# The RMS norm of the memory tokens: spread over partitions by VectorE and a matmul with ones in place of a round trip through DRAM

## The chip, the cores and the metric

The kernel runs on one core of one Trainium2 chip. The metric is the device time of one execution in microseconds (us). Three runs of the kernel before took 786.47, 784.92 and 788.44 us; their median is 786.47 us.

The engines of the core go by the names that the profile gives them: PE is TensorE (matmuls; PEld are its weight loads), DVE is VectorE, ACT is ScalarE, POOL is GpSimd and SP is SyncE. SP and POOL issue most of the DMAs. Each engine works through its own instructions in their order, and waits at one until what it needs is there; waits between engines are semaphores.

## The reference

One block of a hybrid decoder on 512 tokens of width 1024 in float32: a token mixer (SSD heads and causal pooling), a cross-attention into 256 memory tokens, a SwiGLU feed-forward, each with an RMS norm ahead and a residual add behind, and a last RMS norm. What the change touches is the norm of the memory tokens, `rmsnorm(mem, mem_norm)`, which feeds the keys and values of the cross-attention:

```python
def rmsnorm(x, g):
    xf = x.astype(jnp.float32)
    y = xf * lax.rsqrt(jnp.mean(xf * xf, axis=-1, keepdims=True) + EPS)
    return (y * g.astype(jnp.float32)).astype(x.dtype)
...
    k, v = jnp.split(m_in @ w_kv, 2, axis=-1)
...
        h = h + memory_cross_attention(rmsnorm(h, xattn_norm[l]), rmsnorm(mem, mem_norm[l]),
                                       w_q[l], w_kv[l], w_o[l])
```

## The kernel before, in words

**Number format.** Each operand of a large product is split in two parts, a rounded high part (`whi`, `t_xh`, the left half of `t_mn`) and the rest (`wlo`, `t_xl`, the right half of `t_mn`). A product is then three matmuls: high by high, high by low, low by high. For a weight chunk, ScalarE (or VectorE, for chunks named in `FLAGS`) casts the high part (line 282) and VectorE subtracts to get the low part (line 290). The chunks lie in rotating buffers: six for raw weights (`raw`), four for `whi`, five for `wlo`, two each for two kinds of `wq`.

**Strassen products.** The output projection of the mixer's SSD half is one of the products that are computed by seven sub-products f = 1 to 7. Items `y:f` are these; each has two weight chunks of two k-pairs, and 24 matmuls (line 1384) into PSUM tiles `yA`, `yB` or `yC`. Some weights are sums of quadrants. For y:3 the sum is made by DMAs that POOL issues with an add (`sums`, lines 220 and 223): line 223 adds `wq` into `wq`, and the result is what line 282 casts for y:3.

**The order.** `SPEC` is a list of slots, written by hand. Each slot names items. The main loop goes over the slots: for slot t it emits the `post` part of the items of slot t-1, the `prep` part of those of slot t+1, the weight splits for slot t+1, and then the matmuls (`mm`) of slot t. A scheduler orders what it emits on each engine, TensorE in the order of emission.

**The memory tokens.** Two items: `ml` (`i_memld`, line 1118) loads `mem` by rows (`t_rmx`) and its transpose (`t_mem`, eight tiles of 128 channels by 256 tokens), squares the rows on ScalarE with a sum per token, and calls `RmsT.split` (line 434), which makes 1/rms for each token as a column `rm` (128 x 2: token on partition). The transposed tiles need that number along the free dimension, equal on all partitions (`t_rmt`, 128 x 256). With the flag `rmdma`, `split` gets it through DRAM: one DMA writes the column to `d_rm` (line 443), and a second reads it back, broadcast over the partitions (line 445). Both are issued by SP, which also issues the weight loads; the second waits for the first. Without the flag, the rest of `split` and `mm` and `post` of the same class do it on the engines, as they do for `r1`, the norm of the first stage.

The item `mm` (`i_mem`, line 1134) then scales each of the eight tiles (line 1142, VectorE), casts the high part (line 156, ScalarE) and subtracts for the low part (line 157, VectorE) into `t_mn`. `k:1` (`i_k`, line 1172, matmuls of lines 1182 and 1183) is the first product that reads `t_mn`. Its second weight, k.3, gets its low part by a POOL DMA (line 242).

The slots around it are, in order, `y:2.1`, an empty one, `y:5.1 y:6`, `y:3 mm`, `k:1`. So the scaling is emitted with the slot of `k:1`.

The branches of `RmsT` that matter:

```python
            if self.base + "dma" in FLAGS:
                d = dram.tile([n, P], F32, name="d_" + self.base)
                nc.sync.dma_start(d.rearrange("c p -> p c"), p)
                t = self.rt = T(self.base + "t", n=n * P)
                nc.sync.dma_start(t, d.rearrange("c p -> (c p)").unsqueeze(0).broadcast_to([P, n * P]))
                return
            self.rd = T("rd", n=n * P)
            st["spread", self.base] = nc.vector.tensor_tensor(
                                    out=self.rd.rearrange("p (c l) -> p c l", l=P),
                                    in0=ident.unsqueeze(1).broadcast_to([P, n, P]),
                                    in1=p.unsqueeze(2).broadcast_to([P, n, P]), op=ALU.mult)
```

Of the kernel before, what the change touches and what calls it, by code (L numbers as in the profile page):

```python
# [42 lines left out]
START_MM = "10 20 00 11 21 01 12 22 02 13 23 03 24 14 04 15 25 05 16 26 06 17 27 07 a r b c"  # L43

HOLD = 3
FLAGS = ('rmdma', 'Ck.4', 'Ck.3', 'D5.1', 'Cv.2', 'Cv.0', 'Ck.0', 'Cz.6', 'Cz.3', 'D0.0', 'Cz.7', 'D6.1', 'Ck.7', 'yd3', 'D1.1', 'Cv.3', 'yd4', 'Cz.1', 'Cv.4', 'Cq.5', 'Cq.4', 'Cz.5', 'Cq.3', 'Cxbc.11', 'D6.0')
DMA_KEYS = ('q.6', 'xbc.11', 'q.7', 'z.7', 'z.5', 'k.3', 'q.3', 'z.2', 'z.4', 'z.3')
REST = ('g1', 'g0')

# [31 lines left out]
def hybrid_block(ctx: ExitStack, tc: tile.TileContext, a: dict, out: bass.AP,  # L81
# [163 lines left out]
    def split_unit(key):  # L245
# [28 lines left out]
        if key[0] == "s" and f == (6 if CHUNKS[c][0] == "d" else 5):  # L274
            sw[c, "drained"] = st["first rest"] if f == 6 else st.get("drained")
        behind = key[0] == "xbc" and ("free" not in FLAGS or key != plan[1]) and ("spread", "r1") in st
        if "C" + ".".join(str(k) for k in key) in FLAGS:
            cast = nc.vector.tensor_copy(hi[:, :n], raw[:, :n])
# [80 lines left out]
    class Rms:  # L359
# [19 lines left out]
        def mm(self):  # L379
            n = self.n  # L380
            self.ps = PS(self.base)
            if self.parts:
                for i in range(2):
                    nc.tensor.matmul(self.ps[:, :n], ones_r, self.src[i], start=i == 0, stop=i == 1)
            else:
                nc.tensor.matmul(self.ps[:, :n], ones, self.src, start=True, stop=True)

        def post(self):
            n, base, ps = self.n, self.base, self.ps
            y = T(base + "y", n=n)  # L390
            ln = nc.scalar.activation(y, ps[:, :n], AF.Ln, bias=eps)
            after(ln, self.pre)
            nc.scalar.activation(y, y, AF.Exp, scale=-0.5)
            yield
            t = T(base + "t", n=n)
            nc.vector.scalar_tensor_tensor(out=t, in0=ps[:, :n], scalar=eps, in1=y, op0=ALU.add, op1=ALU.mult)
            nc.vector.scalar_tensor_tensor(out=t, in0=t, scalar=-0.5, in1=y, op0=ALU.mult, op1=ALU.mult)
            nc.vector.scalar_tensor_tensor(out=t, in0=t, scalar=1.5, in1=y, op0=ALU.add, op1=ALU.mult)
            st[base,] = t
# [18 lines left out]
    class RmsT:  # L418
# [15 lines left out]
        def split(self):  # L434
# [5 lines left out]
            yield  # L440
            if self.base + "dma" in FLAGS:
                d = dram.tile([n, P], F32, name="d_" + self.base)
# [10 lines left out]
        def mm(self):  # L453
            if self.base + "dma" in FLAGS:
                return
# [3 lines left out]
        def post(self):  # L459
            if self.base + "dma" in FLAGS:  # L460
                st[self.base,] = self.rt
# [6 lines left out]
    def sq_acc(name, src, n=512):  # L468
# [4 lines left out]
        else:  # L473
            sq = T("sq", n=n)
            st[name, "sq"] = nc.scalar.activation(sq, src, AF.Square)
            if f"yd{count[name]}" in FLAGS:
                nc.gpsimd.dma_start(st[name], sq, accum_op=ALU.add)
# [1365 lines left out]
```

## Time and profile before

| what | value |
|---|---|
| median of three runs | 786.47 us |
| the profiled execution | 787.49 us |
| its span, first to last instruction | 785.8 us |
| mean granted TensorE clock | 0.993 |
| HBM read, written | 120.20 MB, 2.13 MB |

The profile is one execution. Its times count from the start of the span. In rows of the timeline the first number is the start in us, the second the duration in us, then engine, line, operation, output and inputs by the program's names, shape and count; in brackets stands the idle time of the engine just ahead, with what ended it. Matmuls are pipelined, so a duration of 0.39 us can stand beside a pace of 0.23 us; the pace is read from the starts. In a row of the view by stretches the busy times of PE, PEld, DVE, ACT and POOL follow the length of the stretch, and behind them stand the granted clock of TensorE, the share of the 16 DMA engines and GB/s.

### The profile page before, as it was taken

To read this page: it belongs to the slowest core of one execution; us is meant where nothing else is said; L and a number is where in the kernel's file an instruction comes from. 1 tells how busy PE (TensorE), PEld (TensorE's weight loads), DVE (VectorE), ACT (ScalarE), POOL (GpSimd) and SP (SyncE) were. 2 spreads that over 40 slices of the span, in tenths; PEclk is the share of its full clock that TensorE was granted. 3 is DMA by queue.
4 is the path that set the end of the run, shared out by engine and by line. 5 is a ranking of instruction groups with operands and counts; after the bars stand their busy time and mean duration, and the time that the engine had idled before them with its cause. 6 is when DMAs were issued, how large, how long until landed. Compare 5 with 4: busy or idle time off the path is not lost.

```text
span 785.8 us, 10551 instructions
## 1 busy us (share of the span) xinstructions
PE 773.9 (98%) x3734; PEld 647.8 (82%) x3734; DVE 646.2 (82%) x1028; ACT 509.3 (65%) x816; POOL 77.6 (10%) x103
## 2 busy tenths in 40 slices
PE   9999999999999989999999999999999999999996
PEld 7788888888888778888888878888888888888985
DVE  5889979989698787667898897789876789867887
ACT  7688788665767356466585597575455666454865
POOL 1000000100001000120210101001101011111010
PEclk9999999999999989999999999999999999999999
DMA  9555743442579886878965966857889786789622
GB/s 331 192 160 151 187 144 93 122 138 84 160 266 240 132 276 195 182 177 257 264 133 126 243 141 190 181 166 159 225 213 270 177 247 156 214 221 244 165 55 107
DMA packets 46676, 145.04 MB, mean 185 GB/s; under 512 B 5472, under 2 KB 7840, under 8 KB 46624
## 3 DMA queue, kind: packets, MB, share of 16 engines
q1 hardware_dynamic: 33952, 100.52, 37.1%
q0 software_dynamic: 12384, 43.52, 31.4%
q8 instruction: 29, 0.48, 0.2%
q10 hardware_dynamic: 288, 0.33, 0.1%
q14 instruction: 23, 0.19, 0.1%
HBM read 120.20 MB, written 2.13 MB: 156 GB/s over the span
## 4 chain that ended last, share of the span: by engine, by line
PE 92%; DVE 4%; DMA 2%; issue 1%; ACT 1%; SPq 0%; DVEq 0%; ACTq 0%
PE gA L1384 15%; PE gB L1384 8%; PE dA L1384 6%; PE gC L1384 4%; PE dB L1384 3%; PE oA L1384 3%; PE xbc L142 2%; PE xbc L141 2%; PE xbc L143 2%; PE vAB L1384 2%; PE k L1182 2%; PE z L141 2%; PE z L143 2%; PE q L141 2%; PE v L141 2%; PE z L142 2%
## 5 line engine op out<-in xcount | busy, mean ns | idle before, releaser
L290 DVE TENSOR_TENSOR wlo<-raw,whi 128x1024 fp32r<-128x1024 f32 (+1 forms) x107 | 128.0, 1206 | 41.9 <-ACT whi L282 40.6
L282 ACT CAST whi<-wq 128x1024 fp32r<-128x1024 f32 (+1 forms) x96 | 99.1, 1034 | 74.9 <-PE gA L1384 11.8
L290 DVE TENSOR_TENSOR wlo<-wq,whi 128x1024 fp32r<-128x1024 f32 (+1 forms) x96 | 114.0, 1199 | 35.4 <-ACT whi L282 34.5
L282 ACT CAST whi<-raw 128x1024 fp32r<-128x1024 f32 x96 | 98.7, 1036 | 60.2 <-PE gA L1384 10.2
L1384 PE MATMUL gA<-whi,t_xh 128*128 128x512 f32 (+1 forms) x240 | 81.4, 373 | 0.0
L1384 PE MATMUL gA<-wlo,t_xh 128*128 128x512 f32 (+1 forms) x192 | 71.4, 372 | 0.0
L202 POOL DMA_DIRECT2D raw<-w_s x42 | 37.1, 884 | 303.0 <-DMA raw<-w_s 209.0
L1384 PE MATMUL gA<-whi,t_xl 128*128 128x512 f32 (+1 forms) x144 | 53.5, 371 | 0.0
L1384 PEld LDWEIGHTS gA<-whi,t_xh 128*128 128x128 f32 x240 | 44.6, 188 | 7.8
L1384 PEld LDWEIGHTS gA<-wlo,t_xh 128*128 128x128 f32 x192 | 36.2, 188 | 6.2
L1384 PE MATMUL gB<-whi,t_xh 128*128 128x512 f32 (+1 forms) x96 | 36.0, 375 | 0.0
L1384 PE MATMUL gB<-wlo,t_xh 128*128 128x512 f32 (+1 forms) x96 | 35.7, 372 | 0.0
L1384 PE MATMUL gB<-whi,t_xl 128*128 128x512 f32 (+1 forms) x96 | 35.7, 371 | 0.0
L1384 PE MATMUL dA<-whi,t_xl 128*128 128x512 f32 (+1 forms) x91 | 34.8, 382 | 0.0
L1384 PE MATMUL dA<-wlo,t_xh 128*128 128x512 f32 (+1 forms) x91 | 34.8, 382 | 0.0
L1384 PE MATMUL dA<-whi,t_xh 128*128 128x512 f32 (+1 forms) x91 | 34.5, 382 | 0.0
L220 POOL DMA_DIRECT2D wq<-raw x22 | 19.7, 895 | 145.8 <-DVE wlo L290 117.7
L1384 PEld LDWEIGHTS gA<-whi,t_xl 128*128 128x128 f32 x144 | 27.1, 189 | 4.6
L1400 ACT ACTIVATE t_gu<-t_gu,r 128x512 f32<-128x512 f32 (+1 forms) x24 | 16.3, 687 | 20.5 <-DVE t_gu L1396 20.5
L141 PE MATMUL z<-t_uh,whi 128*128 128x512 f32 x64 | 25.2, 393 | 0.0
L141 PE MATMUL op<-whi,t_pgh 128*128 128x512 f32 x64 | 25.1, 393 | 0.0
L141 PE MATMUL v<-t_uh,whi 128*128 128x512 f32 x64 | 25.0, 391 | 0.0
(445 smaller groups left out, 2218.3 us busy)
## 6 DMA issues: line engine op xcount, KB each, us to landing
raw<-w_s SPq DMA_DIRECT2D x62, 512.0 KB, 4.8
raw<-w_u SPq DMA_DIRECT2D x52, 512.0 KB, 4.1
wq<-w_s SPq DMA_DIRECT2D x44, 512.0 KB, 4.8
raw<-w_s POOLq DMA_DIRECT2D x40, 512.0 KB, 7.2
wq<-raw POOLq DMA_DIRECT2D x21, 512.0 KB, 6.3
wlo<-raw POOLq DMA_DIRECT2D x10, 512.0 KB, 6.4
wq<-wq POOLq DMA_DIRECT2D x9, 512.0 KB, 8.5
t_abc<-d_acs SPq DMA_DIRECT2D x16, 256.0 KB, 4.6
```

Of the source, the lines that this page charges most:

```text
L141: nc.tensor.matmul(ps, whi, xhi, start=start, stop=False)
L142: nc.tensor.matmul(ps, whi, xlo, start=False, stop=False)
L143: nc.tensor.matmul(ps, wlo, xhi, start=False, stop=stop)
L202: nc.gpsimd.dma_start(sw[c, f][:, :n], quad("11" if f == 7 else "22"), accum_op=ALU.add)
L220: nc.gpsimd.dma_start(sw[c, 6][:, :n], sw[c, 5][:, :n], accum_op=ALU.add)
L282: cast = nc.scalar.copy(hi[:, :n], raw[:, :n])
L290: rest = nc.vector.tensor_tensor(out=lo[:, :n], in0=raw[:, :n], in1=hi.bitcast(F32)[:, :n], op=ALU.subtract)
L1182: nc.tensor.matmul(it.ps[d], wh[:, ws], both, start=k == 0, stop=False, skip_group_check=True)
L1384: nc.tensor.matmul(it.ps[tt][:, o:e], p[:, ts_], w[:, ws], start=first, stop=(c, i, n) == pairs[-1] and p is xh and w is wl, skip_group_ch ...
L1400: st["silu"] = nc.scalar.activation(g, g, AF.Silu, scale=st["r3",][:, c:c + 1])
```

## The change

The flag `rmdma` goes, and the item `mm` moves one slot ahead, between y:5.1 and y:6:

```diff
-FLAGS = ('rmdma', 'Ck.4', 'Ck.3', 'D5.1', ...
+FLAGS = ('Ck.4', 'Ck.3', 'D5.1', ...
...
-    "yr y:2.0 y:5.0", "", "y:1.1", "y:2.1", "", "y:5.1 y:6", "y:3 mm", "k:1", "hg:2 hg:0", "", "k:0 y:7", "", "",
+    "yr y:2.0 y:5.0", "", "y:1.1", "y:2.1", "", "y:5.1 mm y:6", "y:3", "k:1", "hg:2 hg:0", "", "k:0 y:7", "", "",
```

Without the flag, `RmsT.split` ends in the VectorE product shown above (line 448: the identity matrix times the column, 128 x 256, into `t_rd`), and the item has a matmul and a copy of its own:

```python
        def mm(self):
            if self.base + "dma" in FLAGS:
                return
            self.ps = PS(self.base)
            nc.tensor.matmul(self.ps[:, :self.cols * P], ones, self.rd, start=True, stop=True)
...
            t = T(self.base + "t", n=self.cols * P)
            nc.scalar.activation(t, self.ps[:, :self.cols * P], AF.Copy, scale=float(DM))
```

On SP the two DMAs of the round trip stood between the weight loads of line 190, behind the last of the memory tiles' loads; they are gone, and the loads behind them follow the one ahead directly.

On TensorE, at the seam between y:5.1 (`yB`) and y:6 (`yA`), stands a new matmul of the ones with `t_rd`:

```order
L1384 MATMUL yB_2669<-whi_2731,t_xl_2574 128x512
L1384 MATMUL yB_2669<-wlo_2732,t_xh_2561 128x512
L457 MATMUL rm_2780<-t_rd_2592,ones 128x256
L1384 MATMUL yA_2598<-whi_2739,t_xh_2340 128x512
L1384 MATMUL yA_2598<-whi_2739,t_xl_2349 128x512
```

Nothing else moves on TensorE. On VectorE `t_rd` is made right behind the column it spreads, while `ry`, the norm of the mixer's output, is under way:

```order
L415 TENSOR_TENSOR rm<-rm 128x2
L290 TENSOR_TENSOR wlo_2698<-wq_2542,whi_2697 128x1024
L448 TENSOR_TENSOR t_rd_2592<-ident,rm 128x256
L412 TENSOR_TENSOR ry<-ry 128x4
L290 TENSOR_TENSOR wlo_2732<-raw_2544,whi_2731 128x1024
```

Row L448 is new, the others stand as before. Further on, VectorE's scaling of the tiles (L1142) keeps its place behind the adds of `yB`; of the eight tiles the fifth now comes ahead of the weight split for y:3 and the eighth ahead of the last three low parts. On ScalarE the copy out of PSUM (L464) stands ahead of the casts of `t_mn`, and the cast of y:3's second chunk (`whi_2764`) behind three of them, as before:

```order
L241 ACTIVATE wlo_2760<-raw_2729 128x1024
L240 CAST whi_2759<-raw_2729 128x1024
L464 ACTIVATE t_rmt_2807<-rm_2780 128x256
L156 CAST t_mn_2815<-t_mem_2522 128x256
L156 CAST t_mn_2821<-t_mem_2524 128x256
L156 CAST t_mn_2825<-t_mem_2526 128x256
L282 CAST whi_2764<-wq_2542 128x1024
```

Row L464 is the only new one.

More of the change, by code (lines that the diff above doesn't have):

```diff
@@ L45 @@
 HOLD = 3
-FLAGS = ('rmdma', 'Ck.4', 'Ck.3', 'D5.1', 'Cv.2', 'Cv.0', 'Ck.0', 'Cz.6', 'Cz.3', 'D0.0', 'Cz.7', 'D6.1', 'Ck.7', 'yd3', 'D1.1', 'Cv.3', 'yd4', 'Cz.1', 'Cv.4', 'Cq.5', 'Cq.4', 'Cz.5', 'Cq.3', 'Cxbc.11', 'D6.0')
+FLAGS = ('Ck.4', 'Ck.3', 'D5.1', 'Cv.2', 'Cv.0', 'Ck.0', 'Cz.6', 'Cz.3', 'D0.0', 'Cz.7', 'D6.1', 'Ck.7', 'yd3', 'D1.1', 'Cv.3', 'yd4', 'Cz.1', 'Cv.4', 'Cq.5', 'Cq.4', 'Cz.5', 'Cq.3', 'Cxbc.11', 'D6.0')
 DMA_KEYS = ('q.6', 'xbc.11', 'q.7', 'z.7', 'z.5', 'k.3', 'q.3', 'z.2', 'z.4', 'z.3')
```

## The prediction

> **What bounds the kernel now.** I read the page first, then the list of who waited on TensorE, then the chain of waits around the stage that is changed, and last the timeline of single instructions there.
>
> ```profile
> span 785.8 us, 10551 instructions
> PE 773.9 (98%) x3734; PEld 647.8 (82%) x3734; DVE 646.2 (82%) x1028; ACT 509.3 (65%) x816; POOL 77.6 (10%) x103
> PE 92%; DVE 4%; DMA 2%; issue 1%; ACT 1%; SPq 0%; DVEq 0%; ACTq 0%
> ```
>
> TensorE (PE) is busy for 98% of the span and is 92% of the chain that ended last. So a change counts only where it makes TensorE stop, run slower, or do more work. The second view lists all its stops; its columns are the total, the number of times and the longest.
>
> ```profile
> PE yB L1384 <- ACT whi L282: 2.0, 1, 2.0
> PE warm L549 <- DVE ones L120: 1.2, 1, 1.2
> PE yB L1384 <- DVE wlo L290: 0.7, 1, 0.7
> PE hT L1541 <- DVE t_h L1331: 0.2, 1, 0.2
> ```
>
> Four stops in all. The two at yB are neighbours, in the item y:3, and they are the only ones that are not the start or 0.2 us. The chain of waits shows what stands behind them (start, duration, what).
>
> ```profile
> 257.90 8.47 DMA d_rm<-rm
> 266.42 7.46 DMA t_rmt<-d_rm
> 273.90 1.28 DVE t_mem L1142 x3
> 275.18 0.51 DVE t_h L1079
> 275.76 1.09 DVE t_mn L157 x3
> 276.85 0.40 DVE t_mem L1142
> 277.24 1.15 DVE wlo L290
> 278.43 6.34 PE yB L1384 x16
> ```
>
> The memory norm goes out to DRAM and comes back in 15.9 us; VectorE scales the first memory tokens only at 273.90, and behind those the second weight chunk of y:3 is cast late. This is the DMA's 2% of the whole chain. Now what it costs TensorE, from its timeline; each row is one matmul, and those left out follow at an even pace.
>
> ```profile
> 267.68 0.39 PE L1384 MATMUL yA<-whi,t_xh 128*128 128x512 f32 x1
> 273.12 0.39 PE L1384 MATMUL yB<-whi,t_xh 128*128 128x512 f32 x1
> 276.62 0.68 PE L1384 MATMUL yB<-whi,t_xh 128*128 128x512 f32 x1 [1.97 <-ACT whi L282]
> 284.61 0.40 PE L1182 MATMUL k<-t_mn,whi 128*128 128x512 f32 x1
> 287.39 0.39 PE L1182 MATMUL k<-t_mn,whi 128*128 128x512 f32 x1
> 276.77:283.60 6.83, 6.12 (x14) 4.34 (x15) 6.33 (x13) 2.95 (x6) 0.83 (x1) 0.50 0.99 226
> ```
>
> y:6 (yA) has 24 matmuls and takes 273.12 - 267.68 = 5.44 us, 0.227 us each. y:3 (yB) has 24 of the same shape and takes 284.61 - 273.12 = 11.49 us. **The loss is 11.49 - 5.44 = 6.05 us.** The last row, of the view by stretches, explains the larger part: from 276.77 to 283.60 the granted clock (third number from the end) is 0.50. The stops are 2.7 us of the loss; the other 3.4 us are y:3 at half pace.
>
> **The change part by part.** *TensorE gets one matmul more*, rm<-t_rd,ones 128x256, ahead of y:6. The same form runs once at the start, with 512 columns, between even matmuls.
>
> ```profile
> 24.02 0.39 PE L143 MATMUL xbc<-t_xgh,wlo 128*128 128x512 f32 x1
> 24.25 1.02 PE L457 MATMUL r<-t_rd,ones 128*128 128x512 f32 x2
> 24.71 0.80 PE L141 MATMUL xbc<-t_xgh,whi 128*128 128x512 f32 x1
> 25.34 0.40 PE L142 MATMUL xbc<-t_xgl,whi 128*128 128x512 f32 x1
> ```
>
> Without r the row at 25.34 would start two even steps after 24.02, at 24.48; so r costs 0.86 us. I take half of it for half the columns, **+0.43 us**; ends 0.23 (one even matmul) and 0.86.
>
> *VectorE and ScalarE get one instruction each*: t_rd (L448) and the copy out of PSUM (L464).
>
> ```profile
> L448 DVE TENSOR_TENSOR t_rd<-ident,r x1: 692/692/692, 22.8 to 22.8; 128x512 f32<-128x512 f32 x1
> L464 ACT ACTIVATE t_r1t<-r x1: 600/600/600, 25.3 to 25.3; 128x512 f32<-128x512 f32 x1
> 259.56 0.17 DVE L412 TENSOR_TENSOR ry<-ry 128x4 f32<-128x4 f32 x1 [0.56 <-ACT ry L411]
> 267.65 1.06 ACT L240 CAST whi<-raw 128x1024 fp32r<-128x1024 f32 x1 [0.71 <-PE yB L1384]
> 268.10 1.40 DVE L1079 SCALAR_TENSOR_TENSOR t_h<-yB,ry,t_h 128x512 f32<-128x512 f32 x2
> 274.42 1.20 ACT L156 CAST t_mn<-t_mem 128x256 fp32r<-128x256 f32 x3 [5.71 <-DVE t_mem L1142]
> 275.52 1.04 ACT L282 CAST whi<-wq 128x1024 fp32r<-128x1024 f32 x1
> ```
>
> At half the size they take between 0.35 and 0.69, and 0.30 and 0.60 us. t_rd stands just ahead of L412 and so falls into the 0.56 us for which VectorE waits there: cost 0 to 0.13 us on VectorE, nothing on TensorE, which needs t_rd 8 us later. L464 stands behind L240, in 5.7 us of idle ScalarE. Both cost nothing; if that cover were gone it would be at most 0.7 us in the chain below.
>
> *The wait that goes.* rm's matmul runs at 267.68; L240 ends at 268.71, L464 by 269.3, and VectorE has finished its adds at 269.50. So the first t_mem starts at 269.50 instead of 273.90, **4.40 us earlier**. *What is late next?* With the new matmul y:6 runs from 268.11 to 273.55 and y:3 starts then; its second chunk wants whi at 273.55 + 6 x 0.227 = 274.91 and wlo two matmuls later, at 275.36. ScalarE casts the three t_mn by about 271.2 and then whi, which takes the buffer of y:6's first chunk, free after 18 of the 24 matmuls, at 272.2; whi is there at 273.3, 1.6 us early. VectorE does t_mem x3 (1.28), the first yA add (0.75, once y:6's first half is done, about 271.0), t_mn x3 (1.1), t_mem x2 (0.9) and then wlo (1.2): 274.9, half a microsecond early. So y:3 does not stop, and without a stop I expect no half clock: k starts at 273.55 + 5.44 = 278.99.
>
> *Two DMAs less.* What is issued beside them may land sooner, above all L223, the DMA that adds up the weights of y:3's second chunk and without which their cast cannot start.
>
> ```profile
> L223 POOL DMA_DIRECT2D wq<-wq x1: 859/859/859, 259.5 to 259.5; - x1
> DMA to landing us min/median/max: 14.2/14.2/14.2
> wq<-wq POOLq DMA_DIRECT2D x9, 512.0 KB, 8.5
> q0 software_dynamic: 75, 0.31, 92.5%
> q0 software_dynamic: 12384, 43.52, 31.4%
> 266.93 0.58 SPq L190 DMA_DIRECT2D raw<-w_s  x1
> 276.37 1.23 POOL L242 DMA_DIRECT2D wlo<-raw  x1
> DMA to landing us min/median/max: 7.6/7.6/7.6
> ```
>
> L223 lands at 273.7, after 14.2 us, where the median of its kind is 8.5 (third row). Between 257 and 267 the POOL queue's 75 packets took 92.5% of 16 engines' 10 us, 1.97 us each; over the whole run its 12384 took 31.4% of 16 x 785.8 us, 0.32 us each. That is the time of d_rm's write, 256 elements of 4 bytes. I take it that this write held the others up, so that L223 lands by about 268 (259.5 and 8.5) and the cast above is free to run at 272.2. The other end is that L223 stays at 273.7: cast until 274.9, wlo until 276.2, a stop of 0.8 us. The load behind the two removed rows on SP went out at 266.93, right behind them, and can now go as soon as its buffer is free. Its sum on POOL, and behind that L242, which makes the low part of k's second weight, wait for it and move up with it.
>
> **The sum.** -6.05 + 0.43 = **-5.62 us**. Behind k TensorE stops nowhere but for 0.2 us (the fourth stop), and by the code each load there waits for a buffer that compute frees, so loads and work move up together. The profiled execution took 787.49 us (785.8 and 1.7 around it) and would take 781.9; it is 1.0 above the median of the three runs, 786.47, and from that the forecast is 786.47 - 5.62 = **780.9**. The bounds of the matmul alone make it 780.7 to 781.3, and with a median's own uncertainty of some 1.5 us (the runs lie between 784.92 and 788.44) 779.2 to 782.5.
>
> **The rivals.**
>
> *The half clock stays.* If the 0.50 from 276.77 has a cause other than the stop, only the 2.7 us of stops go: 786.47 - 2.7 + 0.43 = 784.2. For it: the stop ahead of it was only 1.97 us. Against it: the slow stretch begins just as that stop ends, and no other stop of this length is there to test it. Chance 0.06. [...]
>
> *The sum for y:3 is late.* L223 still lands at 273.7, the other end above: 780.9 + 0.8 = 781.7. For it: the slow packets are those of the POOL queue, not d_rm's own. Chance 0.08. [...]
>
> *k stops instead.* L242 was issued at 276.37 and landed 7.6 us later, at 284.0; k's second half, which needs it, starts 287.39 - 284.61 = 2.78 us after k, at 281.8 in the new time. Were L242 not to move, TensorE would stop 2.2 us there: 783.1. Against it: the load that L242 queues behind on POOL loses the wait on SP. Chance 0.08.
>
> *Nothing gained.* Another operand of y:3 or k may be as late as the one removed, and hidden behind it so far; then all is lost again but no more: 786.5. In the order I see none: 0.04.
>
> *Slower.* The new matmul stands in TensorE's order in front of y:6, and TensorE takes nothing past it. It stops there if t_rd is not ready at 267.68. If VectorE made t_rd only where it now makes t_mem, at 273.9, TensorE would stop 6.2 us, run at half pace behind it (3.4) and pay the matmul: 786.47 - 6.05 + 6.2 + 3.4 + 0.43 = 790.5. It decides from a t_rd later than 267.7; the order has it ahead of a row that ran at 259.56, 8 us before. Chance 0.03.
>
> **How the numbers follow.** The forecast has 0.71, the rivals 0.06, 0.08, 0.08, 0.04 and 0.03. The range goes from 779.0, the forecast with the run's uncertainty, to 784.3, which takes in the late sum, k's stop and the half clock; outside are the last two rivals and some of the noise. Half a per cent (3.9 us, about what a measurement of this kernel can tell from no change) ends at 782.5. Faster than that: 0.65 of the forecast, 0.06 of the late sum and 0.02 of k's stop, 0.73. Slower: 0.03. Between: 0.24.
>
> **What would show it.** In the changed kernel's profile the list of TensorE's stops has no yB row, or one below 0.5 us; the stretch at clock 0.50 near 277 is gone; rm's matmul costs 0.3 to 0.6 us in the timeline; the first t_mem starts about 4.4 us earlier, at 269 to 270; L223 lands within 9 us; k starts at about 279.0, and all that follows lies 5.6 us earlier. Wrong would be: a yB or rm row of over 1 us in the stops, a k row, or a new stretch at 0.50.

## The result, and the profile after

| | before | changed |
|---|---|---|
| median | 787.61 us (784.92 to 791.84, 10 runs) | 782.59 us (781.84 to 783.32, 10 runs) |
| profiled execution | 787.49 us | 782.21 us |
| its span | 785.8 us | 780.3 us |
| mean granted clock | 0.993 | 0.998 |

The ratio of the times is 0.9934, with a 95% interval of 0.9915 to 0.9953: 5.2 us less, between 3.7 and 6.7. From span to span it is 5.5 us. One execution of the kernel before, which took 1302.81 us at a granted clock of 0.557, is left out of all ratios and counts below.

The page of the changed kernel has TensorE busy for 99% of the span and carrying 96% of the chain that ended last; the 2% that the DMA had there are gone.

```profile
span 780.3 us, 10552 instructions
PE 770.9 (99%) x3736; PEld 646.0 (83%) x3736; DVE 646.5 (83%) x1029; ACT 509.5 (65%) x817; POOL 77.6 (10%) x103
PE 96%; DVE 2%; ACT 1%; issue 1%; DMA 0%; SPq 0%; DVEq 0%; ACTq 0%
```

In the list of TensorE's stops (total, times, longest) both rows of yB are gone; the last row, of 0.2 us at the very start, is new and has nothing to do with the change.

```profile
PE warm L549 <- DVE ones L120: 1.2, 1, 1.2
PE hT L1541 <- DVE t_h L1331: 0.2, 1, 0.2
PE s L579 <- ACT t_xgh L159: 0.2, 1, 0.2
```

TensorE's timeline at the new matmul and at the seams of y:6, y:3 and k:

```profile
267.52 0.39 PE L1384 MATMUL yB<-wlo,t_xh 128*128 128x512 f32 x1
267.75 0.59 PE L457 MATMUL rm<-t_rd,ones 128*128 128x256 f32 x2
...
268.42 0.40 PE L1384 MATMUL yA<-whi,t_xl 128*128 128x512 f32 x1
...
273.67 0.39 PE L1384 MATMUL yB<-whi,t_xh 128*128 128x512 f32 x1
...
279.11 0.39 PE L1182 MATMUL k<-t_mn,whi 128*128 128x512 f32 x1
```

y:3 now takes 279.11 - 273.67 = 5.44 us, as y:6 does, where it took 11.49. From 267.52 to 268.42 two even steps of 0.227 would take 0.45; they take 0.90, so rm's matmul costs 0.45 us. On VectorE and ScalarE (timeline, with the idle time ahead in brackets) the tokens are scaled as soon as the adds ahead are through, and the second chunk of y:3 is cast in time:

```profile
269.48 1.27 DVE L1142 SCALAR_TENSOR_TENSOR t_mem<-t_mem,vec,t_rmt 128x256 f32<-128x256 f32 x3
...
273.61 1.22 DVE L290 TENSOR_TENSOR wlo<-wq,whi 128x1024 fp32r<-128x1024 f32 x1
```

```profile
268.67 0.38 ACT L464 ACTIVATE t_rmt<-rm 128x256 f32<-128x256 f32 x1
...
272.32 1.06 ACT L282 CAST whi<-wq 128x1024 fp32r<-128x1024 f32 x1 [1.13 <-PE yA L1384]
```

The cast at 272.32 waits only for its buffer, not for the sum of line 223 any more. That sum, and the POOL queue's packets between 257 and 267 (packets, MB, share of 16 engines), in the view of the DMA:

```profile
q0 software_dynamic: 288, 1.05, 60.9%
...
raw<-w_s POOLq DMA_DIRECT2D x1, 512.0 KB, 5.1
wq<-wq POOLq DMA_DIRECT2D x1, 512.0 KB, 5.6
```

288 packets in the ten microseconds in place of 75, 0.34 us each in place of 1.97, and the sum lands after 5.6 us in place of 14.2. The stretch in which the clock had been 0.50 is granted in full (third number from the end):

```profile
276.77:283.60 6.83, 6.83 (x38) 5.80 (x37) 6.79 (x13) 3.57 (x6) 0.00 (x0) 1.00 0.67 211
```

What this does not tell: whether the gain comes from the engines' way to make the row, from the slot, or from the DMAs that are gone; and whether the half clock really came from the stop.

### The profile page after: what moved, and what is told of

It is laid out like the page before. It is cut to its first block, busy times and chain, and to the rows that moved or that the text cites. A ratio compares the mean times of both kernels' runs of the same rounds, so it can differ in the third digit from the quotient of the medians.

```text
span 780.3 us, 10552 instructions
## 1 busy us (share of the span) xinstructions
PE 770.9 (99%) x3736; PEld 646.0 (83%) x3736; DVE 646.5 (83%) x1029; ACT 509.5 (65%) x817; POOL 77.6 (10%) x103
## 4 chain that ended last, share of the span: by engine, by line
PE 96%; DVE 2%; ACT 1%; issue 1%; DMA 0%; SPq 0%; DVEq 0%; ACTq 0%
PE gA L1384 15%; PE gB L1384 8%; PE dA L1384 6%; PE gC L1384 4%; PE dB L1384 3%; PE oA L1384 3%; PE yA L1384 3%; PE xbc L142 2%; PE xbc L141 2%; PE xbc L143 2%; PE vAB L1384 2%; PE k L1182 2%; PE op L141 2%; PE z L141 2%; PE op L142 2%; PE op L143 2%
```

## The experiments

All times are medians; ratios are to runs of the kernel before on the same chip, with the 95% interval. The edits are shown shortened; those inside `RmsT` act on `rm` alone.

| run | median us | ratio to before | span us |
|---|---|---|---|
| e1, engines only | 788.48 | 1.0027 (1.0013 to 1.0041) | 785.8 |
| e2, slot only | 786.47 | 1.0008 (0.9991 to 1.0026) | 786.4 |
| e3, changed + write | 787.32 | 1.0000 (0.9981 to 1.0019) | 786.7 |
| e7, DMA a slot earlier | 781.48 | 0.9942 (0.9924 to 0.9960) | 781.1 |
| e8a, write of 8-byte packets | 782.37 | 0.9939 (0.9916 to 0.9961) | 780.5 |
| e8b, write spread out | 782.15 | 0.9939 (0.9916 to 0.9962) | 781.0 |
| e8c, write of 512-byte packets | 782.16 | 0.9937 (0.9914 to 0.9959) | 780.5 |
| e9, layout of the column only | 781.72 | 0.9928 (0.9912 to 0.9944) | 780.4 |
| the changed kernel again, beside e9 | 783.09 | 0.9945 (0.9929 to 0.9961) | 780.6 |
| e4, one stop of 1.2 us | 784.28 | 0.9967 (0.9954 to 0.9981) | 782.2 |
| e4, one stop of 2.0 us | 786.59 | 0.9989 (0.9973 to 1.0006) | 784.5 |
| e4, one stop of 4.0 us | 789.35 | 1.0033 (1.0018 to 1.0047) | 788.7 |

**The two halves of the change, each alone.** e1 takes the flag away and leaves the slot; e2 moves the item and leaves the flag.

```diff
-FLAGS = ('rmdma', 'Ck.4', ...
+FLAGS = ('Ck.4', ...
```

> Half of the change alone: the flag goes (VectorE and the product with ones make the row), the scaling stays in the slot of y:3. In the order the rm matmul then stands behind y:3 on TensorE, directly ahead of k, and the scaling of the tokens behind the last adds of yB. Theory (the round trip was only late, and the slot decides when its replacement is early): y:3 runs without a stop and ends near 279; rm's matmul, the copy out (0.38 us), two adds of yB (1.4), one t_mem (0.43) and one cast (0.4) stand between y:3 and k, so TensorE stops 2 to 5 us at k, and if a stop of 2 us or more is followed by 6.8 us at clock 0.50, 3.4 us more are lost. Against the changed kernel (782.6) plus 2 to plus 8 us: 784.6 to 790.6, no better than before by more than 3 us. Rival (taking the two DMAs away is what gains, the slot is beside the point): 781.5 to 783.5, no stop at k above 0.5 us.

```diff
-"y:5.1 y:6", "y:3 mm", "k:1"
+"y:5.1 mm y:6", "y:3", "k:1"
```

> The other half alone: the round trip through DRAM stays, the scaling moves one slot ahead. TensorE's, POOL's and SyncE's orders are those of before; on VectorE and ScalarE a few rows change places. Theory (the first scaling waits for the DMA, not for its slot): the first t_mem starts at 273 to 275 as before, TensorE stops 1.5 to 2.7 us in y:3, the clock falls to 0.50 behind the first stop, time within 1.5 us of before. Rival (the slot alone brings the gain): the stops of y:3 are below 0.5 us and the time is 781 to 783.

e1 is 0.3% slower than before. y:3 runs through, but TensorE stops ahead of k instead. Its longest stop, the chain of waits there and the stretch at half clock behind it:

```profile
PE k L1182 <- DVE t_mn L157: 3.0, 1, 3.0
```

```profile
278.80 1.40 DVE t_h L1079 x2
280.20 1.19 DVE t_mem L1142 x3
281.39 0.35 DVE t_mn L157
281.87 0.47 PE k L1182
```

```profile
282.85:286.26 3.41, 3.41 (x12) 2.93 (x11) 3.41 (x8) 1.97 (x5) 0.00 (x0) 0.50 0.85 336
```

rm's matmul stands behind y:3 there, so the scaling starts at 280.20, behind the adds of yB, and k waits for its first low part. Half clock follows from 282.85 to 286.26. 3.0 us of stop, 1.7 of half clock, a further stop of 0.3 and the matmul's 0.45 take back 5.45 of the 6.05 us that y:3 gains; its span is that of before all the same, so 0.6 I do not find.

e2 is as before within its interval; its chain is that of before:

```profile
257.85 8.93 DMA d_rm<-rm
266.84 7.47 DMA t_rmt<-d_rm
274.33 0.48 DVE t_mem L1142
```

```profile
PE yB L1384 <- DVE t_h L1079: 2.4, 1, 2.4
```

Its first stop, 2.4 us, is a little longer than that of before and stands at y:3's first matmul: a slot earlier, the scaling that waits for the DMA stands ahead of an add on VectorE that y:3's tile waits for. With the second stop of 0.7 that is 3.1 us, more than the 1.5 to 2.7 I expected.

So neither half brings anything alone: without the slot the row comes too late from the engines, without the engines the slot has nothing to scale with. Both theories hold in their main point.

**Is it the lateness of the round trip, or more?** e3 is the changed kernel plus the old write, which nothing reads; e7 keeps the round trip and starts it a slot earlier.

```diff
+                nc.sync.dma_start(dram.tile([n, P], F32, name="d_rm").rearrange("c p -> p c"), p)
                 self.rd = T("rd", n=n * P)
```

> The changed kernel, plus the write of the 256 elements of 4 bytes to DRAM as before, which nothing reads. Every engine's order is that of the changed kernel, SyncE has the one DMA more. Theory of the prediction (that write held up the POOL queue's packets): the sum of line 223 lands 11 to 15 us after its issue, against 5.6 in the changed kernel and 14.2 before, the POOL queue's packets between 257 and 267 take over 1 us each against 0.34; y:3's second chunk is cast late and TensorE stops 0 to 0.8 us: 782.4 to 783.6, and, if a stop below 1 us is followed by half clock as well, up to 787. Rival (something else made the sum late before, such as the broadcast read or the loads around it): it lands within 7 us, no stop, 782.0 to 783.2.

```diff
-"y:5.1 y:6", "y:3 mm"  ...  "yf:1", "y:1.0 yf:2 yf:3 ml"
+"y:5.1 mm y:6", "y:3"  ...  "yf:1 ml", "y:1.0 yf:2 yf:3"
```

> The round trip through DRAM stays, but the item that loads and squares the memory tokens is named one slot earlier, and the scaling stands where the changed kernel has it. The order of y:1, y:2 and y:5 on TensorE shifts somewhat with it. Theory (the round trip cost only by being late; 15.9 us begun some 5 us earlier end by 269.5): t_rmt is there by 269.5, the stops of y:3 go as in the changed kernel and the added matmul's 0.43 us is not paid: 781.5 to 783.0, the half clock near 277 gone. Rival (the write slows the sums wherever it stands, or the loads that move ahead of the weights make something else late): the sum of line 223 or another lands late, TensorE stops 1 us or more somewhere between 245 and 290, 784 to 789.

e3 gives back the whole gain: 787.32 us, although no engine waits for that write and the row is made in time. The DMA view of its stretch from 257 to 267, and its stops:

```profile
q0 software_dynamic: 70, 0.29, 84.7%
...
raw<-w_s POOLq DMA_DIRECT2D x1, 512.0 KB, 12.9
wq<-wq POOLq DMA_DIRECT2D x1, 512.0 KB, 15.1
raw<-w_s SPq DMA_DIRECT2D x1, 512.0 KB, 13.9
wq<-w_s SPq DMA_DIRECT2D x1, 512.0 KB, 13.8
```

```profile
PE k L1183 <- DMA wlo<-raw: 2.2, 1, 2.2
...
PE yB L1384 <- ACT whi L282: 0.7, 1, 0.7
PE yB L1384 <- DVE wlo L290: 0.5, 1, 0.5
```

The chain of waits ahead of k's stop, and the stretch at half clock behind it:

```profile
261.55 13.87 DMA raw<-w_s
...
276.15 0.54 POOL raw L202
276.68 10.16 DMA wlo<-raw
286.88 0.39 PE k L1183
```

```profile
287.90:291.31 3.41, 3.41 (x13) 2.92 (x12) 0.20 (x1) 0.36 (x1) 0.00 (x0) 0.50 0.96 336
```

All four transfers that were under way beside the write land after 13 to 15 us, where the changed kernel has 5.1, 5.6, 5.9 and 6.0. The sum makes y:3 stop for 1.2 us; the load of SyncE's queue makes the sum behind it on POOL, and with it line 242, late for k, which stops for 2.2 us and then runs 3.41 us at half clock, from 287.90 to 291.31. That is 1.2 + 2.2 + 1.7 = 5.1 us of the 6.4 by which its span is longer than the changed kernel's (0.6 more is a longer stop at the start; 0.7 I do not find). The theory of e3 had the mechanism, but it counted y:3 alone and not k. With the item named a slot earlier (e7), the DRAM route is as fast as the change: 781.48 us, no stop at y:3 or k. Its view of the DMA from 257 to 267 has neither DMA of the round trip, so both go out ahead of it. Between 250 and 257 its DMA engines move 102 GB/s at a share of 0.90, where those of e1, which has no such write, move 282 at 1.01; the four transfers issued from 257 to 267 land after 4.5 to 7.9 us. TensorE stops for none of them. In e7 TensorE's order of y:1, y:2 and y:5 differs somewhat too, so it is no clean test by itself.

**What about the write is slow?** Three runs put other unread writes in its place: the same bytes in 128 packets of 8, the same 256 elements 512 bytes apart, and 64 KB in packets of 512 bytes.

```diff
 e8a: nc.sync.dma_start(dram.tile([P, n], F32, name="d_rm"), p)
 e8b: nc.sync.dma_start(dram.tile([n, P, P], F32, name="d_rm")[:, :, 0].rearrange("c p -> p c"), p)
 e8c: nc.sync.dma_start(dram.tile([P, P], F32, name="d_rm"), self.rd[:, :P])
```

> The changed kernel plus a write of the same 1 KB that nothing reads, as 128 packets of 8 bytes into consecutive places (in e3: 256 packets of 4 bytes; landing 8.5 us, the sum of line 223 landing after 15.1 us, 787.3 us in all). Theory A (each small packet that goes to DRAM costs a fixed time of its own, 8.5 us / 256 = 33 ns): the write lands in some 5 us, the sum of line 223 after 9 to 12 us, and the time lies between 782.5 and 786. Theory B (what counts is that one small region of DRAM is written and the reads wait for the region, however many packets): as in e3, landing 8 us or more, 786 to 788.5. Rival C (any write issued there does it): also as in e3, and then the run with 512 bytes per packet as well.

> The changed kernel plus a write of 256 elements of 4 bytes that nothing reads, each to a place 512 bytes from the next, so no two in the same 512 bytes (in e3 they were consecutive). Theory A (a fixed time for each small packet): as e3, the write lands after 8 to 9 us, the sum of line 223 after 13 to 16 us, 786 to 788.5. Theory B (packets to the same small region are worked through one after the other): the write lands in 2 to 4 us, the sum of line 223 within 8 us, 782 to 783.5.

> The changed kernel plus a write of 64 KB in 128 packets of 512 bytes that nothing reads (half of the spread column, so issued some 2 us later than in e3). Theories A and B (the small packets are what counts): the write lands in 2 to 4 us, the sum of line 223 within 8 us of its issue, no stop of TensorE in y:3 or k above 0.5 us: 782 to 783.5. Rival C (any write to DRAM issued there holds up the reads): the sum lands after 10 us or more, 785 to 788.5.

| write | it lands after, us | line 223 lands after, us | time, us |
|---|---|---|---|
| e3: 256 x 4 bytes, consecutive | 8.5 | 15.1 | 787.32 |
| e8a: 128 x 8 bytes, consecutive | 3.3 | 9.5 | 782.37 |
| e8b: 256 x 4 bytes, 512 bytes apart | 2.3 | 8.3 | 782.15 |
| e8c: 128 x 512 bytes | 4.4 | 8.5 | 782.16 |

e8b decides against a fixed price for each small packet (theory A): as many packets of the same size land in 2.3 us once they lie apart. It also rules out that any write does it, as does e8c. But theory B does not hold as I put it either: e8a writes the same 1 KB and lands in 3.3 us. Over the 2.3 us of e8b, e3's write takes 6.2 us more for 256 packets, 24 ns each, and e8a's 1.0 us more for 128, 8 ns each. What was slow here is 256 packets of 4 bytes to 1 KB on end (8.5 us in e3). Whether that is their size, or the order in which the two columns alternate, these runs do not tell. The sums of e8b and e8c land a little after the 8 us I allowed, and e8c's write after more than 4. That need not be the write's doing: in the runs with no such write line 223 lands after 5.3 to 8.1 us, so the 5.6 of the changed kernel's profile is at the low end.

**The layout alone.** e9 is the kernel before, with the column written token by token as in e8a and read by VectorE in that order. Every engine's order is that of before, and nothing else of the change is in it.

```diff
-                d = dram.tile([n, P], F32, name="d_" + self.base)
-                nc.sync.dma_start(d.rearrange("c p -> p c"), p)
+                d = dram.tile([P, n], F32, name="d_" + self.base)
+                nc.sync.dma_start(d, p)
...
+                m3 = mt.rearrange("q (c p) -> q c p", p=P)
-                nc.vector.scalar_tensor_tensor(out=mt, in0=mt, ..., in1=st["rm",], ...
+                nc.vector.scalar_tensor_tensor(out=m3, in0=m3, ..., in1=st["rm",].rearrange("q (p c) -> q c p", p=P), ...
```

> The kernel before with one thing changed: the column goes to DRAM token by token (128 packets of 8 bytes, as in e8a) instead of column by column (256 of 4 bytes), and VectorE's scaling reads the row in that order. No engine's order changes, no matmul is added, the scaling stays in the slot of y:3. Theory (the loss of before comes from the write of 4-byte elements into one small region, which lands late itself and holds up the reads of the weight sums): the write lands after 3 to 4 us instead of 8.5, the row is back after 7.5 us more or less, at 267 to 269.5, the sum of line 223 lands within 10 us, y:3 does not stop for more than 0.3 us, no half clock: as the changed kernel without its 0.43 us of matmul, 781.3 to 782.5. Rival (the trip through DRAM itself is too slow there, whatever the layout): the first t_mem starts at 271 or later, TensorE stops over 1 us in y:3, 784 to 787.

> The changed kernel once more, beside e9 on the same chip: 782.0 to 783.0. If e9's theory holds, the two lie within half a microsecond of each other, e9 lower by 0.43 at most.

The view of the tile d_rm in e9 has both DMAs (start, time to landing, the write the first):

```profile
L443 SPq DMA_DIRECT2D d_rm<-rm x1: 326/326/326, 258.4 to 258.4; - x1
L445 SPq DMA_DIRECT2D t_rmt<-d_rm x1: 327/327/327, 262.1 to 262.1; - x1
...
DMA to landing us min/median/max: 3.6/5.1/6.5
```

```profile
wq<-wq POOLq DMA_DIRECT2D x1, 512.0 KB, 8.3
```

The row is back at 262.1 + 6.5 = 268.6, the sum of line 223 lands after 8.3 us, y:3 does not stop and no half clock follows: 781.72 us against 783.09 of the changed kernel beside it. The changed kernel lies just above its expectation, and the two are 1.37 us apart where at most 0.43 was expected: the six runs of e9 are 781.17 to 782.18 us, those of the changed kernel 781.61 to 784.00. The matmul's 0.45 is part of that; the rest I do not find, as the spans of the profiled executions, 780.4 and 780.6, differ by 0.2 alone. So e9 is at least as fast as the change, with one layout in place of a rebuilt route. The layout of one 1 KB write was enough to make the loss of before; the change gains because it has no such write and, as e1 shows, because its slot makes the row early enough.

**Does a stop bring the half clock?** In the changed kernel ScalarE copies rm's row back over its operand N times, and a second rm matmul reads it; a dependence for the order alone holds all of y:6 and y:3 behind that matmul. TensorE then has one stop, of a length that N sets, with no DMA near its cause.

```diff
             nc.tensor.matmul(self.ps[:, :self.cols * P], ones, self.rd, start=True, stop=True)
+            for _ in range(N):
+                nc.scalar.copy(self.rd, self.ps[:, :self.cols * P])
+            nc.tensor.matmul(self.ps[:, 256:512], ones, self.rd, start=True, stop=True)
```

> As e4_stop4 with two copies instead of four, so the stop should be 1.1 to 1.3 us long. If the half clock needs a stop near 2 us, no stretch at 0.50 follows and the time is 782.4 + 0.45 + 1.2 = 784.0; if any stop of over a microsecond does it, 3.4 us at 0.50 follow and it is 785.7. The other runs' stops below 0.8 us were followed by none.

> The changed kernel with one stop of TensorE and nothing else in its way: behind rm's matmul ScalarE copies the row back over its operand four times, and a second rm matmul reads that, ahead of all of y:6. The stop should be 1.6 to 2.3 us long. Theory (a stop of about 2 us is followed by 3.4 us or twice that at clock 0.50, as behind the 1.97 us of before, the 2.2 us of e3 and the 3.0 us of e1): a stretch at 0.50 begins within 2 us of the stop's end, and the time is 782.6 + 2.0 + 0.45 + 1.7 or 3.4 = 786.7 to 788.5. Rival (the clock fell for another cause, such as the DMA traffic there): no stretch at 0.50, 784.5 to 785.5. If y:3 stops too, because its casts now stand behind the copies, that adds its own length.

> As e4_stop4 with nine copies, so the stop should be 3.7 to 4.2 us long. Theory (3.41 us at clock 0.50 behind a stop of 2 to 3 us, twice that where a second stop falls into it): one or two stretches of 3.41 us, 782.4 + 0.45 + 3.9 + 1.7 or 3.4 = 788.5 to 790.2. Rival (a longer stop is punished in proportion): over 7 us at 0.50, above 791.

The stop in each, from its list of stops, with two, four and nine copies:

```profile
PE rm L457 <- ACT t_rd L457: 1.2, 1, 1.2
```

```profile
PE rm L457 <- ACT t_rd L457: 2.0, 1, 2.0
```

```profile
PE rm L457 <- ACT t_rd L457: 4.0, 1, 4.0
```

And the stretches by clock (third number from the end), first with two copies, then four, then nine:

```profile
268.00:285.00 17.00, 15.85 (x75) 13.16 (x75) 15.34 (x29) 8.93 (x17) 1.76 (x2) 1.00 0.85 234
```

```profile
271.06:274.48 3.42, 3.42 (x10) 2.65 (x9) 2.68 (x7) 1.71 (x5) 0.00 (x0) 0.50 1.04 254
```

```profile
271.96:278.79 6.83, 5.80 (x14) 4.57 (x15) 3.81 (x10) 3.70 (x10) 0.00 (x0) 0.50 1.03 196
```

1.2 us is followed by no half clock, 2.0 us by 3.42 us of it, 4.0 us by 6.83 us, which here begins within the stop. The spans follow the sum: 780.3 + 0.45 for the second matmul + the stop + half of what TensorE is busy in the slow stretch (3.42 and 5.80 us) gives 782.0, 784.5 and 787.7; measured are 782.2, 784.5 and 788.7 (the last has 0.4 us more of small stops at the start, and 0.6 that I do not find). So in these runs the stop is the cause, and where half clock follows, it adds 1.7 us to the 2.0 of the stop. It does not always follow: with four copies, three of the ten executions have a mean granted clock of 0.997 or 0.998 and spans of 782.7 to 782.9 us, which is the sum without half clock (782.75); the other seven have 0.994 or 0.995 and spans of 784.5 to 786.0. Their median, 786.59 us, lies just under what I expected. With two copies none of the nine is below 0.996.

## Why the prediction was right, and where it was not

- **The loss in y:3** (6.05 us: 2.7 of stops, 3.4 of half clock) was read rightly: y:3 takes 5.44 us, exactly as forecast.
- **The matmul** costs 0.45 us, forecast 0.43. **t_rd** ran at 260 and **the copy** at 268.67; TensorE waited for neither.
- **The first scaling** starts at 269.48, forecast 269.50. The cast of y:3's second chunk ends at 273.4 (forecast 273.3) and its low part at 274.8 (274.9), ahead of TensorE's need at 275.0 and 275.5.
- **The half clock** goes with the stop: the rival in which it stays falls with the 1.00 in the changed kernel's stretch, and e4 shows that a stop alone brings it (2.0 us of stop, 3.42 us at 0.50).
- **The sum**: -5.62 forecast, -5.5 from span to span, -5.2 by the ratio. The forecast of 780.9 is 1.7 us below the median of 782.59, and the base was the step that was off. The 6.05 us were read from an execution of 787.49 us with two pieces of half clock of 3.41 us; they were taken from a median of three, 786.47, which by the groups in the last point of this list is the time of an execution with one piece (the clocks of those three are not on record). One piece is worth 1.7 us: 786.47 - 6.05 + 1.7 + 0.43 = 782.55. The profiled execution's own time with the same sum gave 781.9, and the profiled execution of the changed kernel took 782.21.
- **What went wrong in the rivals: the price of the late sum.** I put it at 0.8 us, with only y:3 to pay, and k's stop at 2.2 us as a separate case, without half clock. e3 shows that they are one case: the write that holds the sum (15.1 us to landing) holds the load behind it too (13.9), and both, with the half clock behind k's stop, cost 4.7 us against the changed kernel's median. Had the change kept that write, it would have gained nothing, at 787.3 rather than the 781.7 I wrote. The working credited the gain to the wait that goes; e3 shows that ending the wait gains nothing as long as the write holds up the other transfers, and e9 that one cause, the write's layout, made both. The forecast assumed that the write held up the sum, and its number rests on that assumption, which it priced too low and had no run to show; that the same edit removed both was in part luck. No run has the late row alone, without the other transfers held up, so what the wait alone costs stays open.
- **"Nothing gained"** had 786.5 and another operand as late as the one removed. e3 has such an operand, k's low weight part, which the prediction had named in its rival of k's stop. In the changed kernel it is in time, because the same edit removed its cause.
- **What I did not forecast**: the runs of before lie 6.9 us apart, those of the changed kernel 1.5. In the profiled executions half clock came in pieces of 3.41 or 3.42 us, or twice that, each worth 1.7 where TensorE is busy throughout, and their mean granted clock goes with the number of pieces: 0.993 with two, 0.995 with one, 0.997 to 0.999 with none. By that clock, from which the pieces of the others are estimated, the 62 executions of before that ran beside the experiments fall into three groups that do not overlap:

| mean granted clock | pieces | executions | time, us | median, us |
|---|---|---|---|---|
| 0.997 and more | none | 17 | 784.35 to 785.92 | 785.05 |
| 0.995 | one | 23 | 785.95 to 787.39 | 786.73 |
| 0.994 and less | two | 22 | 787.50 to 789.73 | 788.39 |

The steps are the 1.7 us of a piece. So most of the spread of before is half clock that comes or stays away, and the profiled execution is of the dearest kind. What decides it, these runs do not tell.

## What to carry to other kernels

When a small DMA stands in the chain of waits, look at what else was under way beside it: if the packets of other queues take several times their usual time there (here 1.97 us against 0.32 over the whole run), the DMA's price is paid in more than one place, and taking away only the wait on it may gain nothing (e3: 787.32 us, a ratio of 1.0000). Before rebuilding such a transfer on the engines, try its layout (e9: 781.72 us), or its place some microseconds earlier (e7: 781.48 us). And look for half clock behind a stop of TensorE: here the stop of 2.0 us cost 3.7 with it, in seven of ten executions, and the one of 1.2 us only its length, by the mean clocks in all nine. Before you take a loss from a median, see that both are of the same kind of execution: here the mean granted clock told them apart (0.993 with two pieces of half clock, 0.995 with one).

## What the runs showed of the hardware that was not expected

- 256 packets of 4 bytes to consecutive places in DRAM landed after 8.5 us and brought the four transfers beside them, of SyncE's queue and of POOL's, from 5 or 6 us to 13 to 15; the same number 512 bytes apart landed after 2.3 us and left line 223 at 8.3. In e3 the POOL queue had 70 packets in ten microseconds, at 1.94 us each, in place of the changed kernel's 288 at 0.34; no run here shows which part stalls.
- Half clock came in lengths of 3.41 us or twice that: 6.83 in before and e2, 3.41 in e1 and e3, 3.42 and 6.83 with stops of 2.0 and 4.0 us. It followed a stop of 1.97 us in the profiled execution of before and, by the mean clocks, one of 2.0 us in seven of ten executions, and one of 1.2 us in none of nine.
